# A fused attention and feed-forward step on one core: softmax-merge statistics on GpSimd, factor loads on SyncE, and the last merges inside the first output-projection block

## The chip, the cores and the metric

The kernel runs on one core of one Trainium2 chip. The metric is the device time of one execution in microseconds (us). The program is one launch of some 39,000 instructions on five engines, each of which works through its own instructions in order: TensorE (PE in the profile), VectorE (DVE), ScalarE (ACT), GpSimd (POOL) and SyncE (SP). SyncE issues most DMA transfers, ScalarE a few.

## The reference, cut to what matters

One layer for a prompt of 2048 positions and eight short samples: RMSNorm, one combined input projection, eight heads of attention with three dilated branches, a spatial gating unit, one output projection with a residual, and a SwiGLU feed-forward. All is in float32. What the change touches is the merge of the branches, per position and head:

```python
def _layer_prompt(x, biases, ...):
    q, k, v, u, vg = _project(x, norm1_g, w_in)
    for (w, d), bias_hj in zip(BRANCHES, biases):
        o, l = _dilated_prompt(q, k, v, bias_hj, d, w // d + 1)
        outs.append(o); lses.append(l)
    att = _merge_branches(outs, lses)
    ...
    x = x + jnp.concatenate([att, u * gate], axis=-1) @ w_out
    x = x + _swiglu(x, norm2_g, w_gate, w_up, w_down)

def _merge_branches(outs, lses):
    w = jax.nn.softmax(jnp.stack(lses, axis=0), axis=0)
    return jnp.sum(w[..., None] * jnp.stack(outs, axis=0), axis=0)
```

The kernel computes the two narrow branches together as a "band" and the widest one (distance 16) as a "strided" part, and merges the two results with two factors per position.

## The kernel before, in words

A float32 product is made of three products of high and low halves (`qh`, `ql`; `ph`, `pl`; `woh`, `wol`), so nearly every operand on its way to TensorE is split: ScalarE writes the high half, VectorE or GpSimd subtracts it.

**Phases.** The input projection ends about 599 us into the span. Then come the eight heads, until about 946 us; then the first block of the output projection (six tiles of 128 rows, the function `first_block`), and the feed-forward with its three blocks, which fills the rest.

**Attention items.** Each head has 20 items: 16 bands (128 queries against up to 640 keys) and 4 strided items (512 queries). One item is started per *step*; steps are counted from `B0`. A planner, `at(step, phase, function)`, sorts all the small functions by step, and within a step by phase (early, exp, low, scores, turn, mid, values, out, misc, store). That sorted list is the order of the instructions on every engine. A band takes: score matmuls (L881), the bias on VectorE (L887), the exponential on ScalarE (L892), transposes (L900), the copy of the high half `ph` (L903, ScalarE) and of the low half `pl` (L922, VectorE), and the product with the values (L936). A strided item has the like, with a max subtraction on GpSimd (`e`, L962), queries put in order by GpSimd (`qo`, L865), and its product with the values `v` at L985 and L986; ScalarE copies its result `o` out at L993. Items of a head follow a written list: `FIRST` for head 0, `OTHER` for heads 1 to 6, `LAST` for head 7.

**Merging a head.** When a head's items are over, during the next head's first steps, `Stats` spreads the strided sums (L1006, `sm`), sums them on TensorE (L1012) and copies them back (L1015). `Weights` forms the two factors (a minimum, a subtraction, an exponential, a product, a sum, a reciprocal, a product: L1030 to L1041), turns them (L1045) and stores them to a scratch array in memory, `f_d` (L1050, L1051). `merge_load` reads them back, spread over all partitions, in four chunks of 512 positions (`pair<-f_d`, L1061, issued on ScalarE's queue; `raw` and `zn`, L1065, on SyncE's queue for the last chunks). `merge` takes three instructions of GpSimd per chunk (L1072, L1074, L1076), one per step, and `merge_store` writes the rows of the head to `cat_d` (L1081).

**Loads of a head.** `load_head` issues on SyncE: `qh`, `k` and `ql` (L825, 1 MB each), the bias `b` (L830), and the values, `ve` for the bands (L836 or L845) and `v` for the strided items (L841, eight transfers). Head 0 does so during the end of the projection; head 1's loads begin at step 1 of head 0.

**Queues.** SyncE issues in order: a transfer that must wait (for its buffer, its data, or for the last transfer on its completion counter) holds all behind it. There are eight counters, taken in turn by the transfers of SyncE and ScalarE together.

**The first block.** Rows of `cat_d` are loaded per tile of 128 positions (`load_cat`, L1359) and split (`split_cat`, L1366 to L1370: a sum of halves into a staging tile `raw`, a copy on ScalarE, a subtraction on VectorE). The order of the tiles is 1, 2, the last slice of 1, 2 and 0, then 3, 4, 5 (first half of the columns), then the second half of the columns for all tiles, with weights `half1` (`fr<-in_w_out_dram`, 8 loads, L1332) that are split by ScalarE and GpSimd (L135, L138). `tick()` counts half tiles, and `later(n, ...)` puts work at such a tick.

Of the kernel before, what the change touches and what calls it, by code (L numbers as in the profile page):

```python
# [19 lines left out]
P = 128  # L20
T = 2048
# [44 lines left out]
def hymba_step(ctx: ExitStack, tc: tile.TileContext, A: dict, O: dict):  # L66
# [933 lines left out]
    class Stats:  # L1000
        def __init__(self, h, st):
            self.h, self.st = h, st["t"]

        def a(self):
            self.m = ap_.tile([P, 2 * P], F32, name="sm", tag="sm", bufs=1).rearrange("p (a r m) -> p a r m", a=2, m=RUN)
            dve.tensor_tensor(self.m, self.st[:, 4:6].unsqueeze(3).broadcast_to([P, 2, NT, RUN]),  # L1006
                              sel_m.unsqueeze(1).unsqueeze(1).broadcast_to([P, 2, NT, RUN]), op=OP.mult)
# [9 lines left out]
    class Weights:  # L1017
        def __init__(self, stats, n0=0, n1=NT):
            self.h, self.t, self.n0, self.n = stats.h, stats.st[:, :, n0:n1], n0, n1 - n0
# [7 lines left out]
        def weights_a(self):  # L1027

            self.f = f = self.small("f", 3)
            dve.tensor_tensor(f[:, 2, :], self.t[:, 0], self.t[:, 1], op=OP.min)  # L1030
            dve.tensor_sub(f[:, 0:2, :], self.both(f[:, 2:3, :]), self.t[:, 0:2])
            act.activation(f[:, 0:2, :], f[:, 0:2, :], AF.Exp)

        def weights_b(self):
            f, m = self.f, self.f[:, 2, :]
            dd = self.small("dd", 2)
            dve.tensor_mul(dd, f[:, 0:2, :], self.t[:, 2:4])
            dve.tensor_add(m, dd[:, 0, :], dd[:, 1, :])
            dve.reciprocal(m, m)
            self.w = w_ = self.small("w", 2)  # L1040
            dve.tensor_mul(w_, f[:, 0:2, :], self.both(self.f[:, 2:3, :]))  # L1041

        def turn(self):
            self.p = pt = ps_a()
            pe.transpose(pt[0:2 * self.n, 0:P], self.w.rearrange("p a t -> p (a t)"), ident)  # L1045

        def store(self):
            n = 2 * self.n
            rows = ap_.tile([2 * NT, P], F32, name="fr", tag="fr", bufs=2)[0:n]
# [6 lines left out]
    def merge_load(h, ch):  # L1056

        if h < H - 2 or h == H - 2 and ch < 2:
            f = pair_tile(F32)
            mf[h, ch] = (f[:, 0], f[:, 1])  # L1060
            act.dma_start(f, dap(f_d, h * 2 * T + ch * 512, [[0, P], [T, 2], [1, 512]]))  # L1061
# [55 lines left out]
    FIRST = list(range(8)) + ["s", 8, 9, "s", 10, 11, "s", 12, "s", 13, 14, 15]  # L1117
# [29 lines left out]
    for h in range(1, H):  # L1147

        s0 = B0 + (h - 1) * NI
        at(s0 + 1, "misc", begin, h)  # L1150
        for y in (1, 2, 3, 4, 10, 12):
            at(s0 + y, "misc", load, h)
        at(s0 + 16, "misc", order_bias, h)
    def stats_of(h, steps):
        d = {}
        at(*steps[0], lambda: d.update(s=Stats(h, sts[h])))
# [4 lines left out]
    def weights_of(d, steps, n0=0, n1=NT):  # L1161
        w = {}
        at(*steps[0], lambda: w.update(w=Weights(d["s"], n0, n1)))
        for (y, ph), fn in zip(steps, "weights_a weights_b turn store".split()):
            at(y, ph, lambda fn=fn: getattr(w["w"], fn)())

    def steps_of(s0, *steps):
        return [(s0 + y, ph) for y, ph in steps]

    for h in range(H):  # L1170
# [4 lines left out]
        if end:  # L1175

            x = s0 - NI
            d = stats_of(h, steps_of(x, (11, "misc"), (12, "early"), (13, "early")))
            weights_of(d, steps_of(x, (14, "early"), (14, "misc"), (16, "early"), (16, "exp")), 0, NT // 2)
            at(x + 17, "mid", merge_load, h, 0)  # L1180
            at(x + 17, "mid", merge_load, h, 1)
            for part in range(3):
                at(x + 19 + part, "store", merge, h, 0, dve, part)
                at(x + 20 + part, "store", merge, h, 1, pool, part)
            weights_of(d, steps_of(s0, (3, "early"), (4, "early"), (5, "early"), (5, "early")), NT // 2, NT)
        else:
            d = stats_of(h, steps_of(s0, (2, "misc"), (3, "misc"), (4, "early")))
            weights_of(d, steps_of(s0, (4, "misc"), (5, "misc"), (6, "turn"), (6, "mid")))

            for ch, (a, b) in enumerate(((8, 11), (8, 14), (14, 17), (20, 23) if ahead else (17, 20))):  # L1190
                at(s0 + a, "mid", merge_load, h, ch)
                for part in range(3):
                    at(s0 + b + part, "store", merge, h, ch, pool, part)
            if ahead:
                at(s0 + 17, "store", merge_store, h, 0, 2)
                at(s0 + 27, "store", merge_store, h, 2, 4)
            else:
                at(s0 + 23, "store", merge_store, h, 0, 4)
# [153 lines left out]
    def load_cat(B, i, a, b, place=None):  # L1352
# [7 lines left out]
        B.late[i, a] = (ch, cl, a, b)  # L1360

    def split_cat(B, i, a=0, staged=raw_tile):
        ch, cl, a, b = B.late.pop((i, a))
        m = max(a, 4)
        x = staged()[:, 0:(b - m) * P].rearrange("p (s t) -> p s t", t=P)
        dve.tensor_add(x, cl[:, m:b].bitcast(F32), ch[:, m:b].bitcast(F32))  # L1366
        for y0, y1, src in ((a, m, cl[:, a:m].bitcast(F32)), (m, b, x)):
# [424 lines left out]
    at(L + 1, "misc", split_cat, B, 0, 0, lambda: ap_.tile([P, 512], F32, name="m0", tag="m0", bufs=1))  # L1792
# [65 lines left out]
    def first_block(B):  # L1858

        places = {0: None, 1: acc_place(2), 2: acc_place(4)}  # L1860
# [5 lines left out]
        merge_load(h, 2)  # L1866
        merge_load(h, 3)
# [5 lines left out]
        load_cat(B, 4, 0, KD)  # L1873
        load_cat(B, 5, 0, KD)
        half1_load(*range(KD))
        sync.dma_start(gain[0], dap(A["final_g"], 0, [[0, P], [1, D]]))
        plan.run(10 ** 9)
        split_cat(B, 1)
        split_cat(B, 2)
        for n, what in ((2, [(merge, h, 2, pool), (merge, h, 3, pool), (split_cat, B, 1, KD - 1), (split_cat, B, 2, KD - 1)]),  # L1880
# [252 lines left out]
```

## Time and profile before

| what | value |
|---|---|
| median of 3 runs | 2623.61 us (2622.35 to 2627.72) |
| the profiled execution, its own time | 2621.67 us |
| its span in the profile | 2619.9 us |
| TensorE busy in the span | 2490.8 us (95%) |
| VectorE, ScalarE, GpSimd busy | 1425.6, 1221.1, 1370.9 us |
| the part that the change touches | about 590 to 1020 us of the span |
| TensorE busy in it | 386.16 of 430 us |

The time of the execution is 1.8 us more than the span. "Busy" of TensorE includes time in which its clock was granted at half speed, so the idle time alone doesn't say how much could be won. A row of waits names the engine and line that waited, what ended the wait last, the sum, the count and the longest. In a timeline each row has the start, the duration, the engine, the line, the output and input, and in brackets the idle time before it.

### The profile page before, as it was taken

Reading aid. Unit: us, or ns where it says so; the run is one execution under the profiler, and the core shown is the slowest. Engines: PE = TensorE matmul, PEld = TensorE weight load, DVE = VectorE, ACT = ScalarE, POOL = GpSimd, SP = SyncE. Lnnn points to the kernel's source line nnn. Section 1 sums busy time; section 2 is a strip of 40 time slices with the busy share of each in tenths; the row PEclk is TensorE's granted clock in tenths of the full one; section 3 lists DMA queues with packets and bytes.
Section 4 is the critical chain, followed back from the end, with each engine's and each line's share of the span. In section 5 each row is a group of like instructions: output and inputs, shape, how many; then the busy total and the mean of one; then the engine's idle time right before and its main releaser. Section 6 shows DMA issues by size and latency. Waiting matters only on the chain. (4 is left out here: it accounts for less than half of the span.)

```text
span 2619.9 us, 38931 instructions
## 1 busy us (share of the span) xinstructions
PE 2490.8 (95%) x13583; PEld 2202.5 (84%) x13583; DVE 1425.6 (54%) x2808; ACT 1221.1 (47%) x2570; POOL 1370.9 (52%) x1042
## 2 busy tenths in 40 slices
PE   8999899998999989999999999999999999999997
PEld 6777687677888868889989988999999987999996
DVE  3359686345888856444344465344444466444445
ACT  6424344445778746454554545332333336434332
POOL 2035754133567656776766743454554534666662
PEclk9999999999999989999999999899999999999999
DMA  8764844688677674464554664554453643655553
GB/s 245 224 203 153 279 147 129 183 263 241 187 227 226 165 217 141 155 194 146 181 177 133 197 177 140 169 186 172 152 210 129 224 148 125 200 198 195 198 199 110
DMA packets 313875, 481.06 MB, mean 184 GB/s; under 512 B 25907, under 2 KB 178916, under 8 KB 307792
## 3 DMA queue, kind: packets, MB, share of 16 engines
q1 hardware_dynamic: 301116, 455.90, 54.2%
q10 hardware_dynamic: 12564, 22.68, 3.3%
q8 instruction: 108, 1.77, 0.3%
q14 instruction: 87, 0.71, 0.1%
HBM read 382.76 MB, written 165.84 MB: 209 GB/s over the span
## 5 line engine op out<-in xcount | busy, mean ns | idle before, releaser
L1571 POOL TENSOR_TENSOR op<-fr,op 128x512 fp32r<-128x512 f32 x385 | 488.5, 1299 | 308.2 <-ACT op L1567 263.7
L1628 PE MATMUL ps_m<-xh,op 128*128 128x384 f32 (+4 forms) x1932 | 618.5, 320 | 3.8 <-DVE zn L1649 3.8
L1630 PE MATMUL ps_m<-xh,op 128*128 128x384 f32 (+4 forms) x1932 | 618.2, 320 | 1.7 <-POOL op L1571 1.7
L1629 PE MATMUL ps_m<-xl,op 128*128 128x384 f32 (+4 forms) x1932 | 617.3, 320 | 0.0
L1701 PE MATMUL ps_o<-dw,hw 128*128 128x512 f32 x2040 | 486.2, 393 | 18.2 <-DVE acc L1703 16.9
L1701 PEld LDWEIGHTS ps_o<-dw,hw 128*128 128x128 f32 x2040 | 380.4, 188 | 102.3 <-DVE acc L1703 24.0
L1628 PEld LDWEIGHTS ps_m<-xh,op 128*128 128x128 f32 x1932 | 371.9, 192 | 8.3 <-issue 2.8
L1629 PEld LDWEIGHTS ps_m<-xl,op 128*128 128x128 f32 x1932 | 371.6, 192 | 3.5
L1630 PEld LDWEIGHTS ps_m<-xh,op 128*128 128x128 f32 x1932 | 371.6, 192 | 2.0 <-POOL op L1571 2.0
L1703 DVE TENSOR_TENSOR acc<-acc,ps_o 128x512 f32<-128x512 f32 (+1 forms) x362 | 246.9, 686 | 215.1 <-PE ps_o L1701 215.0
L1668 ACT ACTIVATE ps_t<-zn 128x384 f32<-128x384 f32 (+1 forms) x126 | 58.3, 463 | 476.0 <-DVE zn L1651 370.4
L1567 ACT ACTIVATE op<-fr 128x512 fp32r<-128x512 f32 x396 | 235.4, 623 | 24.2 <-DMA fr<-ab_d 13.5
L138 POOL TENSOR_TENSOR dw<-fd,dw 128x1024 fp32r<-128x1024 f32 x66 | 158.7, 2405 | 123.3 <-ACT dw L135 123.1
L318 PE MATMUL ps_s<-wh,xh 128*128 128x512 f32 x480 | 198.4, 413 | 6.3 <-ACT xh L135 6.1
L319 PE MATMUL ps_s<-wl,xh 128*128 128x512 f32 x480 | 192.8, 402 | 1.7 <-DVE wl L226 1.7
L320 PE MATMUL ps_s<-wh,xl 128*128 128x512 f32 x480 | 192.3, 401 | 0.0
L1571 POOL TENSOR_TENSOR op<-pair,op 128x512 fp32r<-128x512 f32 x63 | 81.5, 1302 | 117.3 <-ACT op L1567 117.3
L1678 ACT ACTIVATE hw<-ps_t 128x384 fp32r<-128x384 f32 (+1 forms) x126 | 56.1, 453 | 175.3 <-DVE ps_t L1674 174.4
L318 PEld LDWEIGHTS ps_s<-wh,xh 128*128 128x128 f32 x480 | 93.0, 194 | 36.4 <-issue 8.2
L320 PEld LDWEIGHTS ps_s<-wh,xl 128*128 128x128 f32 x480 | 93.2, 194 | 20.8 <-DVE xl L138 0.2
L319 PEld LDWEIGHTS ps_s<-wl,xh 128*128 128x128 f32 x480 | 93.5, 195 | 20.2 <-DVE wl L226 2.6
L611 POOL TENSOR_TENSOR vl<-kv,vh 100x512 fp32r<-100x512 f32 (+1 forms) x32 | 46.1, 1440 | 109.9 <-ACT vh L605 35.7
(470 smaller groups left out, 4805.1 us busy)
## 6 DMA issues: line engine op xcount, KB each, us to landing
fr<-ab_d SPq DMA_DIRECT2D x308, 256.0 KB
fd<-in_w_down_dram SPq DMA_DIRECT2D x66, 512.0 KB
out_ks_dram<-in_cache_k_dram SPq DMA_DIRECT2D x56, 512.0 KB
out_vs_dram<-in_cache_v_dram SPq DMA_DIRECT2D x56, 512.0 KB
ab_d<-fr SPq DMA_DIRECT2D x88, 256.0 KB
raw<-in_w_in_dram SPq DMA_DIRECT2D x72, 256.0 KB
qk_d<-pair SPq DMA_DIRECT2D x64, 256.0 KB
ab_d<-pair SPq DMA_DIRECT2D x63, 256.0 KB
```

What stands on the lines that cost most here:

```text
L138: (eng_lo or pool).tensor_sub(lo, src, hi.bitcast(F32))
L318: pe.matmul(o[j], xh[:, k, :], wh, start=(k == 0), stop=False)
L319: pe.matmul(o[j], xh[:, k, :], wl, start=False, stop=False)
L320: pe.matmul(o[j], xl[:, k, :], wh, start=False, stop=(k == KD - 1))
L1567: act.activation(ops[f, j][0], ab[f][j], AF.Copy)
L1571: (pool if f or j in POOL_LOW else dve).tensor_sub(lo_, ab[f][j], hi.bitcast(F32))
L1628: pe.matmul(out, wh[:, ks], xh[:, :, k], start=(k == 0), stop=False)
L1629: pe.matmul(out, wh[:, ks], xl[:, :, k], start=False, stop=False)
L1630: pe.matmul(out, wl[:, ks], xh[:, :, k], start=False, stop=(k == 3))
L1668: act.activation(g, c, AF.Silu)
L1701: pe.matmul(ps[0:nr], l_, r_[:, cs], start=(z == 0 and y == 0), stop=(z == FC - 1 and y == len(pairs) - 1))
L1703: dve.tensor_add(B.acc[i][0:nr, cs], B.acc[i][0:nr, cs], ps[0:nr])
```

## The change

It has four parts.

1. **Statistics on GpSimd, and later.** For heads 0 to 6 five small operations (`sm`, the subtraction of `f`, the product `dd`, its sum, and `w`) go from VectorE to GpSimd. The minimum, the reciprocal and the copy of the sums stay on VectorE, the exponential on ScalarE. All are spread over more steps: the sums start at step 3 instead of 2, and the factors are stored at step 10 instead of 6. Head 7 keeps VectorE.
2. **Factor loads on SyncE, merges later.** The 26 loads `pair<-f_d` go from ScalarE's queue to SyncE's. The merges of a head start at steps 16, 19, 22 and 25 (before: 11, 14, 17, 20), its store is at 28 (before: 23).
3. **Head 0.** Its strided items come after bands 9, 11, 13 and 15 (before: after 7, 9, 11 and 12); head 1's loads start at step 6 instead of 1.
4. **The end.** Both early merges of head 7 are on GpSimd (one was on VectorE). Chunks 2 and 3 of head 6, which were merged during head 7, are merged in the first block, ahead of those of head 7; the second half of head 7's factors is turned and stored at tick 2 of the block instead of before it. The loads of tiles 4 and 5, the `half1` weights and `final_g` move behind head 6's store and head 7's factor loads. The split of tile 0 is in two parts.

```diff
         def a(self):
-            dve.tensor_tensor(self.m, self.st[:, 4:6].unsqueeze(3).broadcast_to([P, 2, NT, RUN]),
+            self.eng.tensor_tensor(self.m, self.st[:, 4:6].unsqueeze(3).broadcast_to([P, 2, NT, RUN]),
...
-            act.dma_start(f, dap(f_d, h * 2 * T + ch * 512, [[0, P], [T, 2], [1, 512]]))
+            sync.dma_start(f, dap(f_d, h * 2 * T + ch * 512, [[0, P], [T, 2], [1, 512]]))
...
-    FIRST = list(range(8)) + ["s", 8, 9, "s", 10, 11, "s", 12, "s", 13, 14, 15]
+    FIRST = list(range(10)) + ["s", 10, 11, "s", 12, 13, "s", 14, 15, "s"]
...
-            d = stats_of(h, steps_of(s0, (2, "misc"), (3, "misc"), (4, "early")))
-            weights_of(d, steps_of(s0, (4, "misc"), (5, "misc"), (6, "turn"), (6, "mid")))
+            d = stats_of(h, pool, steps_of(s0, (3, "misc"), (5, "early"), (6, "early")))
+            weights_of(d, steps_of(s0, (6, "misc"), (7, "early"), (7, "misc"), (8, "early"), (8, "misc"), (10, "early"), (10, "mid")))
+            chunks = ((13, 16), (13, 19), (19, 22), (22, 25))
...
     def first_block(B):
...
-        merge_load(h, 2)
-        merge_load(h, 3)
+        plan.run(10 ** 9)
+        split_cat(B, 1, 0, KD - 1)
+        split_cat(B, 2, 0, KD - 1)
         B.place()
...
-        load_cat(B, 4, 0, KD)
-        load_cat(B, 5, 0, KD)
-        half1_load(*range(KD))
...
-        for n, what in ((2, [(merge, h, 2, pool), (merge, h, 3, pool), (split_cat, B, 1, KD - 1), (split_cat, B, 2, KD - 1)]),
-                        (3, [(split_cat, B, 0, KD - 1), (split_cat, B, 3)]),
-                        (4, [(merge_store, h, 2, 4)]), (5, [(split_cat, B, 4), (open_end, B, 1)]),
+        for n, what in ((2, [(w.turn, lambda: ps_t(1)), (w.store, zn_tile), (merge_load, h - 1, 2), (merge_load, h - 1, 3)]),
+                        (3, [(split_cat, B, i, KD - 1) for i in (1, 2, 0)]),
+                        (4, [(merge, h - 1, 2, pool), (merge, h - 1, 3, pool), (merge_store, h - 1, 2, 4), (merge_load, h, 2), (merge_load, h, 3),
+                             (more_loads,), (split_cat, B, 3)]),
+                        (5, [(split_cat, B, 4), (open_end, B, 1)]),
+                        (6, [(merge, h, 2, pool), (merge, h, 3, pool), (merge_store, h, 2, 4), (half1_split, B, 0, 1)]),
```

What SyncE issues around head 0 (the rows are in the order of its queue; `-` stood there before, `+` stands there now):

```order
 L634 DMA cs_d<-zn 4x512
 L358 DMA v_d<-pair 128x1024
-L825 DMA qh<-qk_d 128x1x2048
 L350 DMA out_vp_dram<-zn 128x512 x2
-L825 DMA k<-qk_d 128x1x2048
 L358 DMA v_d<-pair 128x1024 x2
 L836 DMA ve<-v_d 128x6x128
+L841 DMA v<-v_d 16x16x128 x8
+L825 DMA qh<-qk_d 128x1x2048
+L825 DMA k<-qk_d 128x1x2048
 L825 DMA ql<-qk_d 128x1x2048
-L841 DMA v<-v_d 16x16x128 x8
```

Head 0's `v` now stands ahead of all three large loads of head 1.

GpSimd in the first steps of head 2, where the statistics of head 1 fall due, before:

```order
L1076 TENSOR_TENSOR ob<-ob,o_5763 128x512
L962 TENSOR_TENSOR e_6504<-e_6504,st 128x512
L865 COPY qo<-qh 128x512
L865 COPY qo<-ql 128x512
L962 TENSOR_TENSOR e_6637<-e_6637,st 128x512
L865 COPY qo<-qh 128x512
L865 COPY qo<-ql 128x512
L1072 TENSOR_TENSOR ob<-ob,pair 128x512
```

The same engine at the same kind of place now:

```order
L962 TENSOR_TENSOR e_6497<-e_6497,st 128x512
L1006 TENSOR_TENSOR sm<-st,sel_m 128x256
L1080 TENSOR_TENSOR o_5775<-o_5775,pair 128x512
L865 COPY qo<-qh 128x512
L865 COPY qo<-ql 128x512
L1082 TENSOR_TENSOR ob<-ob,o_5775 128x512
L1078 TENSOR_TENSOR ob<-ob,pair 128x512
L1031 TENSOR_TENSOR f<-f,st 128x32
L1080 TENSOR_TENSOR o_5775<-o_5775,pair 128x512
L1039 TENSOR_TENSOR dd<-f,st 128x32
L1040 TENSOR_TENSOR f<-dd 128x16
L1082 TENSOR_TENSOR ob<-ob,o_5775 128x512
```

The statistics of a head now run between the merge instructions of the head before it (`ob` and `o` with a factor; L1078, L1080 and L1082 are the old L1072, L1074 and L1076).

SyncE in the first block, behind the loads for tiles 0 to 2, before (`xl`, `xh` are the rows of a tile from `cat_d`, first tile 3, then 4 and 5; `acc` the residual rows of tiles 1 and 0):

```order
L1065 DMA raw<-f_d 128x512
L1065 DMA zn<-f_d 128x512
L1359 DMA xl_9904<-cat_d 128x128
L1359 DMA xh_9903<-cat_d 128x128
L1359 DMA xl_9904<-cat_d 128x8x128
L1359 DMA xh_9903<-cat_d 128x4x128
L1321 DMA acc_9909<-in_x_prompt_dram 128x1024
L1321 DMA acc_9911<-in_x_prompt_dram 128x1024
L1359 DMA xl_9904<-cat_d 128x8x128
L1359 DMA xh_9903<-cat_d 128x4x128
```

And now, from the same residual rows on, down to the load of tile 4:

```order
L1333 DMA acc_9895<-in_x_prompt_dram 128x1024
L1333 DMA acc_9897<-in_x_prompt_dram 128x1024
L1071 DMA raw<-f_d 128x512
L1071 DMA zn<-f_d 128x512
L1071 DMA raw<-f_d 128x512
L1071 DMA zn<-f_d 128x512
L1087 DMA cat_d<-ob 64x1024 x2
L1071 DMA raw<-f_d 128x512
L1071 DMA zn<-f_d 128x512
L1071 DMA raw<-f_d 128x512
L1071 DMA zn<-f_d 128x512
L1371 DMA xl_9890<-cat_d 128x8x128
```

The factor loads of head 6 stand behind the residual rows, and tile 4 behind head 6's store (`cat_d<-ob`), which waits for the last of six GpSimd merge instructions, and behind head 7's four factor loads. The residual row `acc_9895` shares its completion counter with the store of head 7's factors on ScalarE's queue, and waits for it.

111 lines of the change are left out of this document (62 added, 49 removed).

## The prediction

> **What bounds the kernel now.** I read the totals first, then the busy time by stretches, then what TensorE waited for in each stretch, then the timelines of those places. The totals and the stretches (length, then busy time of TensorE, its weight loads, VectorE, ScalarE, GpSimd, then TensorE's granted clock):
>
> ```profile
> PE 2490.8 (95%) x13583; PEld 2202.5 (84%) x13583; DVE 1425.6 (54%) x2808; ACT 1221.1 (47%) x2570; POOL 1370.9 (52%) x1042
> 800.00:850.00 50.00, 47.02 (x347) 44.23 (x345) 43.31 (x98) 39.79 (x95) 33.72 (x34) 0.97 0.79 227
> 920.00:940.00 20.00, 14.21 (x83) 11.95 (x82) 17.26 (x26) 12.41 (x31) 18.91 (x14) 0.88 0.75 190
> 940.00:960.00 20.00, 15.95 (x62) 12.22 (x62) 8.07 (x13) 3.63 (x8) 7.06 (x6) 0.84 0.54 155
> ```
>
> TensorE bounds the whole. In the heads VectorE is nearly as full (43.31 of 50 us), and GpSimd has room on average. At the end of attention TensorE is least busy, and GpSimd is full from 920 to 940. What TensorE waited for from 590 to 660, from 660 to 900 and from 900 to 1020 (sum, times, longest):
>
> ```profile
> PE ps_o L985 <- DMA v<-v_d: 5.2, 1, 5.2
> PE ps_t L900 <- DVE el L922: 1.4, 1, 1.4
> PE ps_o L900 <- DVE el L922: 1.0, 1, 1.0
> ...
> PE ps_o L936 <- ACT o L993: 4.4, 3, 2.0
> PE ps_t L1012 <- DVE pl L922: 3.4, 3, 1.4
> PE ps_o L1012 <- DVE pl L922: 1.9, 2, 1.1
> ...
> PE ps_t L900 <- DVE pl L922: 3.3, 2, 2.7
> PE ps_m L1380 <- DVE accm L1370: 3.3, 1, 3.3
> ```
>
> Waits are followed by stretches at half clock (the column 0.50):
>
> ```profile
> 631.40:638.20 6.80, 6.80 (x33) 6.80 (x33) 3.19 (x7) 2.79 (x6) 3.00 (x4) 0.50 1.22 222
> 706.50:709.90 3.40, 3.40 (x17) 3.40 (x16) 2.39 (x6) 2.16 (x5) 0.19 (x1) 0.50 0.96 235
> 733.80:737.20 3.40, 3.40 (x12) 2.81 (x13) 2.57 (x12) 1.16 (x4) 1.48 (x3) 0.50 1.02 393
> 812.10:815.50 3.40, 3.40 (x12) 2.83 (x12) 2.82 (x13) 2.32 (x7) 0.94 (x2) 0.53 1.04 352
> 853.10:856.50 3.40, 3.40 (x13) 3.16 (x12) 3.13 (x12) 2.29 (x7) 0.07 (x1) 0.53 1.03 286
> 935.20:942.00 6.80, 4.74 (x18) 4.29 (x19) 6.62 (x14) 1.68 (x4) 5.43 (x4) 0.50 0.77 195
> 955.70:962.50 6.80, 5.52 (x13) 4.38 (x14) 6.05 (x7) 0.72 (x3) 6.52 (x5) 0.50 1.08 335
> ```
>
> A busy microsecond at half clock loses half of itself: 3.4 us in the first row, 1.7 in each of the four rows of 3.40, 2.4 and 2.8 in the last two. The change is priced stage by stage, waits and clock together.
>
> **Term 1, head 0.** SyncE's timeline before:
>
> ```profile
> 600.69 1.19 SPq L825 DMA_DIRECT2D qh<-qk_d  x1
> 617.96 0.37 SPq L836 DMA_DIRECT2D ve<-v_d  x1
> 618.97 5.68 SPq L841 DMA_DIRECT2D v<-v_d  x8
> ```
>
> Head 0's `v` is issued late (618.97), and its first user waits 5.2 us for it. Head 1's `qh` (600.69) and `k`, 1 MB each, are issued ahead, in the time of the stores to `v_d` that `ve` waits for, and probably take bandwidth from them. The change takes both loads out of the way and puts two more bands, some 4 us of work at 2 us a step, ahead of the first strided product. Either would nearly do. The 5.2 us go, and the 3.4 us of half clock with them: 8.6. What is late next is VectorE, which these items already made wait 1.4 and 1.0 us. I take 8.6 - 2.4, so **6** (3 to 8.6).
>
> **Term 2, heads 1 to 6.** Loads on ScalarE's queue hold its copy `o`:
>
> ```profile
> 703.08 1.45 ACTq L1061 DMA_DIRECT2D pair<-f_d  x2
> 704.57 0.60 ACT L993 ACTIVATE o<-ps_o 128x512 f32<-128x512 f32 x1 [2.37 <-issue]
> ```
>
> The 4.4 us on `o` L993 go, and the 1.7 of half clock at 706.5. On SyncE I cost the 26 loads at nothing: they are due three steps (6 us) behind their store and three ahead of the merge. The head's store at step 28, which waits for the last merge, now stands ahead of the next `v`; those are needed some twelve steps later, which is the cover. The longer path to the factors meets merges that start five steps later too. The products of the statistics (L1012) waited 3.4 + 1.9 us in five heads behind VectorE, with three stretches of half clock (733.8, 812.1, 853.1) of 1.7: 10.4. They now go into TensorE's order at the start of a step instead of its end, a step and a bit behind `sm`, and VectorE has less to do:
>
> ```profile
> L1006 DVE TENSOR_TENSOR sm<-st,sel_m 128x256 f32<-128x256 f32 x6 | 5.8, 968 | 0.0
> L1031 DVE TENSOR_TENSOR f<-f,st 128x32 f32<-128x32 f32 x6 | 1.9, 314 | 0.2
> ```
>
> Up to 6.1 + 10.4 = 16.5 can go. Against it stands GpSimd. The groups of it from 660 to 900, six heads, and the products of the statistics by time:
>
> ```profile
> L1076 POOL TENSOR_TENSOR ob<-ob,o 128x512 f32<-128x512 f32 x24 | 31.2, 1300 | 0.5
> L962 POOL TENSOR_TENSOR e<-e,st 128x512 f32<-128x512 f32 x26 | 27.3, 1049 | 56.1 <-PE ps_t L900 34.1 <-DVE st L961 15.0 <-PE ps_o L900 7.0
> L865 POOL CAST qo<-qh 128x512 fp32r<-128x512 f32 x26 | 16.0, 614 | 0.0
> L854 POOL COPY bp<-b 128x640 f32<-128x640 f32 x6 | 7.9, 1316 | 0.0
> L1012 PE MATMUL ps_t<-sel_n,sm x16: 231/263/374, 733.6 to 890.8; 128*128 128x16 f32 x16
> ```
>
> 733.6 to 890.8 are four heads, so 39.3 us a head and 1.97 a step. In steps 16 to 27 GpSimd has twelve merge instructions (12 x 1.3 = 15.6), one `bp` (1.3), and three strided items (3 x (1.05 + 2 x 0.61) = 6.8): 23.7 us in twelve steps of 1.97 = 23.6. That was so before too, but now the statistics come on top. Their cost on GpSimd isn't in the trace: `sm` has half the columns of L962, hence some 0.55; the four small ones lie between nothing and L962's 1.05, and I take the 0.31 of the row L1031, which is one of them on VectorE. That makes 1.8, with ends of 0.5 and 4.8. So GpSimd gets about 2 us late at the end of the stretch, just where ScalarE's exponential needs `f` and VectorE's reciprocal needs the sum; both are in order, with the copies `ph` and `pl` for TensorE behind them. Of 2 us some 0.7 is covered by the distance of the phases. I charge 1.3 a head, 8 in six. **Term 2 is 16.5 - 8, about 8** (-6 to 16).
>
> **Term 3, end of attention.** VectorE merged a chunk of head 7, and one of its instructions there took 1.74 us:
>
> ```profile
> 934.77 1.74 DVE L1074 TENSOR_TENSOR o<-o,zn 128x512 f32<-128x512 f32 x1
> ```
>
> The wait of 2.7 us for `pl` and the half clock from 935.2 (2.4) lie right behind. Three merge instructions leave VectorE; the split of tile 0, cut in two, is the same work, and the gap between its halves is filled by the items' copies. GpSimd has as many chunks as before in the stretch. **5** (2 to 6).
>
> **Term 4, first block.** Rows of before, from GpSimd, SyncE, ScalarE, VectorE and TensorE:
>
> ```profile
> 953.39 1.27 POOL L1072 TENSOR_TENSOR ob<-ob,raw 128x512 f32<-128x512 f32 x1 [12.68 <-DMA raw<-f_d]
> 958.02 1.59 POOL L1072 TENSOR_TENSOR ob<-ob,raw 128x512 f32<-128x512 f32 x1
> 960.97 1.40 POOL L1076 TENSOR_TENSOR ob<-ob,o 128x512 f32<-128x512 f32 x1
> ...
> 941.34 7.92 SPq L1359 DMA_DIRECT2D accm<-cat_d  x4
> 949.30 0.43 SPq L1065 DMA_DIRECT2D raw<-f_d  x1
> ...
> 946.11 0.58 ACTq L1051 DMA_DIRECT2D f_d<-fr  x1
> ...
> 966.02 0.39 PE L1378 MATMUL ps_m<-op,xh 128*128 128x512 f32 x1
> 981.66 0.39 PE L1378 MATMUL ps_m<-op,xh 128*128 128x512 f32 x1
> ```
>
> 69 products in 15.64 us are 0.227 us each, 24 of them a half tile (5.45). Counted from the first product of tile 1, TensorE without waits is at the last slice of tile 0 at +10.9, at tile 3 at +11.6, at tile 4 at +17.0. Now the chain that feeds them. The factors of head 7 are turned after 12 products (+2.7), and their store is issued at about +3.6. Before, a store issued at 946.11 let SyncE go on at about 948.0 (the four loads end at 949.26, three issues of 0.43 behind the release). So +5.6, and then, at 0.45 an issue, two residual rows and head 6's factors at +7. They took 4.1 us (949.30 to 953.39); behind 1 MB of residual rows I take 5, so GpSimd starts at +12. By the rows its first merge instruction is done 1.3 later, its fourth 6.2, its sixth 9.0.
>
> The staging tile for tile 0's last slice waits for the first instruction (+13.3; split by +14.4, a wait of 3.5), that of tile 3 for the fourth (+18.2; split by +19.6 against +15.1, 4.5). Tile 4's load stands behind the store that waits for the sixth (+21), two issues of 0.55 and four of 0.47: +24, landed and split by +30, against +27: 3. These are 11 us, and three stretches of half clock of about 2 each: 17. What goes is the 3.3 us on L1380 and its 2.8 at half clock, 6. **Term 4 is -11** (-22 to 0).
>
> **Sum.** 6 + 8 + 5 - 11 = 8 us. From the profiled execution, 2621.67, this gives 2613.7; the median of the runs lies 1.9 above that execution. I predict **2614**.
>
> [...]
>
> **Rivals.**
> - *GpSimd becomes the bound of the heads* (slower). Place: the subtraction `f` and the sum on GpSimd, due at steps 6 and 7. If `f` and the sum are late by 2 us each time and TensorE then waits 2.6 in all and drops its clock (1.7), a head loses 4.3, six lose 26: 16.5 - 26 = -9.5 for term 2, and 6 - 9.5 + 5 - 11 = -9.5: **2631**. It decides from 3.6 us a head on. For it: 23.7 of 23.6 us. Against: the L962 row's 56.1 us of idle time ahead.
> - *The first block's queue costs more.* If the factors land at +16 and tile 4 takes 8 us from its issue (twice the 4.1 above), the waits are 7.5, 4.5 and 6.6 and term 4 is -19: **2622**.
> - *Half clock doesn't follow the waits.* Without the four short stretches term 2 is about 1: **2621**. [...]
> - *GpSimd stays hidden, or the first block's waits hide one another* (each makes the next one's need later). One of the two: **2604**.
>
> **How the numbers follow.** Forecast 0.38 (2607 to 2618), hidden costs 0.22, the queue 0.17, the clock 0.08, GpSimd as the bound 0.15. The range 2601 to 2629 leaves out most of the last and the edge of the second. A measurement of this kernel can tell about 0.2% (5.2 us) from no change, here 2618.4 to 2628.9: faster 0.60, same 0.25, slower 0.15.
>
> **What would show it.** Term 1: no wait of L985 for `v` near 631. Term 2: no waits on `o` L993 or at the statistics' products; instead some for the exponential and the reciprocal behind GpSimd, and a head of about 38 us instead of 39.3. Term 3: 920 to 940 fuller. Term 4: SyncE's residual row waits for ScalarE's store, GpSimd starts about 12 us after the first product of tile 1, and TensorE waits at tiles 0, 3 and 4. I am wrong if the heads don't shorten, or if the first block loses less than 5 us or more than 20.

## The result and the profile after

Over 20 runs each, the changed kernel takes 2624.25 us (2619.62 to 2633.17) and the kernel before 2622.59 us (2610.49 to 2629.59). The ratio is 1.0015, with a 95% interval of 1.0001 to 1.0029: no change by the bound of 0.2%, and if anything slower. I had forecast 2614. The profiled execution of the changed kernel has a span of 2621.9 us.

Where the time went is read best from one event that both kernels have in the same order: the copies of the band result `ob` on ScalarE, four per head, and behind them the first product of tile 1 in the first block and the first product of its second half (`woh`). Two such rows of before, the second copies of heads 1 and 6:

```profile
679.51 0.60 ACT L945 ACTIVATE ob<-ps_o 128x512 f32<-128x512 f32 x1
877.39 0.60 ACT L945 ACTIVATE ob<-ps_o 128x512 f32<-128x512 f32 x1
```

The same two in the changed kernel:

```profile
669.81 0.60 ACT L945 ACTIVATE ob<-ps_o 128x512 f32<-128x512 f32 x1
863.76 0.60 ACT L945 ACTIVATE ob<-ps_o 128x512 f32<-128x512 f32 x1
```

Such times, from one profiled execution of each kernel (before, changed, and four of the experiments below; the rows of "from there" and "to" are lengths):

| event | before | changed | part 3 | parts 1, 2 | part 4 | parts 1 to 3 |
|---|---|---|---|---|---|---|
| head 0, first `ob` | 616.08 | 616.50 | 618.60 | 618.36 | 618.90 | 622.50 |
| head 1, second `ob` | 679.51 | 669.81 | 673.60 | 677.86 | 683.22 | 675.70 |
| from head 0's first `ob` to that | 63.43 | 53.31 | 55.00 | 59.50 | 64.32 | 53.20 |
| five heads, to head 6's second `ob` | 197.88 | 193.95 | 199.81 | 192.90 | 197.15 | 194.03 |
| from there to tile 1's first product | 70.52 | 73.80 | 71.61 | 77.13 | 66.35 | 79.50 |
| from there to the second half | 34.43 | 54.42 | 33.17 | 34.46 | 53.68 | 33.96 |

The first row differs by up to 6.4 us, although what TensorE computes up to there is the same in all six. So absolute times of different kernels are not compared below, only lengths from one event to the next.

The change wins 10.1 us from the first `ob` to head 1 (9.7 from the start of the span), 3.9 in five heads, loses 3.3 up to the first block and 20.0 in it. By the second half it is 9.6 us late. Some 8 us of that come back in this pair of profiles behind 1640 us, where nothing was changed; the last section says what that is.

**Head 0.** The wait for `v` is gone (from 590 to 660 no wait of TensorE in the changed kernel is longer than 1.0 us). Before, two stretches at a clock of 0.50 stood there, 6.8 us each, from 631.4 and from 651.9; in the changed kernel one of 3.4 us at 0.50 is left, from 635.1.

**The five heads.** The five heads as one stretch, before and in the changed kernel:

```profile
679.51:877.39 197.88, 183.78 (x1337) 172.90 (x1337) 171.72 (x390) 154.53 (x362) 124.89 (x126) 0.97 0.77 224
669.81:863.76 193.95, 180.26 (x1337) 165.99 (x1337) 164.97 (x365) 153.76 (x362) 129.80 (x149) 1.00 0.79 223
```

TensorE's busy time is the second number, its granted clock the third from the end. It does the same 1337 products. Its idle time, length less busy time, is 14.1 us before and 13.7 now, so the waits bring 0.4; its busy time is 3.5 us shorter, and the clock, 0.97 before, is full. What TensorE waited for in these two stretches, before:

```profile
PE ps_o L936 <- ACT o L993: 4.4, 3, 2.0
PE ps_t L1012 <- DVE pl L922: 3.4, 3, 1.4
PE ps_t L900 <- DVE el L922: 2.7, 10, 0.6
PE ps_o L1012 <- DVE pl L922: 1.9, 2, 1.1
PE ps_o L900 <- DVE el L922: 1.1, 5, 0.4
```

And in the changed kernel:

```profile
PE ps_t L900 <- DVE el L922: 3.8, 10, 0.5
PE ps_t L1012 <- POOL sm L1006: 2.3, 3, 0.8
PE ps_o L900 <- DVE el L922: 1.8, 5, 0.5
PE ps_t L900 <- ACT e L892: 1.6, 5, 0.4
PE ps_t L1051 <- DVE pl L922: 1.5, 3, 0.5
PE ps_o L1051 <- DVE pl L922: 1.0, 2, 0.5
PE ps_o L900 <- ACT e L892: 0.8, 2, 0.4
PE ps_o L1012 <- POOL sm L1006: 0.8, 1, 0.8
```

The waits on `o` and for VectorE at L1012, 9.7 us, have gone, and others of 9.8 us stand in their place: for GpSimd at L1012 (3.1), at the turn of the factors, L1051 (2.5), for `e` (2.4), and 1.8 more for `el`.

**The end.** The waits from 900 to 1020 in the changed kernel:

```profile
PE ps_m L1392 <- ACT xh L1383: 14.1, 2, 8.0
PE ps_m L1394 <- DVE xl L1384: 3.6, 2, 2.9
PE ps_o L985 <- ACT o L993: 2.6, 1, 2.6
PE ps_t L1051 <- DVE w L1047: 1.9, 1, 1.9
```

The first two rows are the first block: 17.7 us, where before had 3.3 on L1380. The stretches from 920 on:

```profile
920.00:940.00 20.00, 17.45 (x102) 14.35 (x101) 14.65 (x26) 11.79 (x27) 12.21 (x10) 1.00 0.61 158
940.00:960.00 20.00, 12.00 (x49) 9.18 (x48) 4.72 (x9) 2.25 (x6) 4.83 (x4) 0.81 0.61 188
960.00:980.00 20.00, 10.23 (x27) 6.80 (x27) 5.75 (x6) 1.89 (x3) 10.52 (x9) 0.67 0.75 177
```

From 940 to 980 TensorE is busy for little more than half (22.23 of 40 us), at a clock of 0.81 and 0.67.

### The profile page after: what moved, and what is told of

It reads as the page before. It is cut to its first block, busy times and chain, and to the rows that moved or that the text cites. A ratio compares the mean times of both kernels' runs of the same rounds, so it can differ in the third digit from the quotient of the medians.

```text
span 2621.9 us, 38941 instructions
## 1 busy us (share of the span) xinstructions
PE 2480.9 (95%) x13583; PEld 2188.5 (83%) x13583; DVE 1414.6 (54%) x2770; ACT 1221.5 (47%) x2570; POOL 1382.9 (53%) x1080
## 5 line engine op out<-in xcount | busy, mean ns | idle before, releaser
L1715 PEld LDWEIGHTS ps_o<-dw,hw 128*128 128x128 f32 x2040 | 381.1, 189 | 102.1 <-DVE acc L1717 23.8
```

What stands on the lines that cost most here:

```text
L1715: pe.matmul(ps[0:nr], l_, r_[:, cs], start=(z == 0 and y == 0), stop=(z == FC - 1 and y == len(pairs) - 1))
```

## The experiments

All changes are against the kernel named. Every ratio is to the kernel before, run in the same session. "Stretch" is the time from tile 1's first product to the first product of the second half.

**The parts one by one.** Part 3 alone, on the kernel before:

```diff
-    FIRST = list(range(8)) + ["s", 8, 9, "s", 10, 11, "s", 12, "s", 13, 14, 15]
+    FIRST = list(range(10)) + ["s", 10, 11, "s", 12, 13, "s", 14, 15, "s"]
-        at(s0 + 1, "misc", begin, h)
+        at(s0 + (6 if h == 1 else 1), "misc", begin, h)
...
+            y = int(h == 0)
+            d = stats_of(h, steps_of(s0 + y, (2, "misc"), (3, "misc"), (4, "early")))
```

> The kernel before with part 3 alone (head 0's strided items and head 1's loads later; head 0's statistics and merges one step later, since its last item now ends later). Theory 1, each part acts in its own place: the wait for v near 631 and its half clock go, head 1 starts about 9.7 us earlier as in the trace of the changed kernel, and nothing is given back: about 9 us faster in the median (6 to 11). Rival, the clock and the order of the items give it back in the heads: head 1 starts earlier, and tile 1's first product less than 4 us earlier; under 4 us faster.

Measured: 2608.81 us (2603.61 to 2613.05) against 2619.21, ratio 0.9954 (0.9936 to 0.9973): 12 us faster by the ratio, above the forecast of 9. In the profile the way from the first `ob` to head 1 is 8.4 us shorter (head 1 itself is only 5.9 earlier, since this execution reached the first `ob` 2.5 us later). The five heads take 1.9 more, the way to tile 1 takes 1.1 more, and the stretch is 1.3 shorter. That is 6.7 us; the rest comes behind the places of the change, so the profile places only part of what the many runs show.

Parts 1 and 2 alone:

```diff
-            d = stats_of(h, steps_of(s0, (2, "misc"), (3, "misc"), (4, "early")))
+            d = stats_of(h, pool, steps_of(s0, (3, "misc"), (5, "early"), (6, "early")))
...
-            act.dma_start(f, dap(f_d, h * 2 * T + ch * 512, [[0, P], [T, 2], [1, 512]]))
+            sync.dma_start(f, dap(f_d, h * 2 * T + ch * 512, [[0, P], [T, 2], [1, 512]]))
...
+        if ahead:
...
+            chunks = ((10, 12), (10, 15), (14, 18), (20, 23))
+        else:
...
+            chunks = ((13, 16), (13, 19), (19, 22), (22, 25))
```

> The kernel before with parts 1 and 2 alone (statistics of heads 0 to 6 on GpSimd and later, factor loads on SyncE, merges later; head 6's four chunks stay in head 7, the first block and head 0 as before). Theory 1: five heads, from the second copy of the band result of head 1 to that of head 6, take 2 to 5 us less than the 197.9 us of before, since throttle-free heads take 38.7 to 39.5 us in both kernels; 0 to 5 us faster in all. Rival, the statistics on GpSimd are what costs the 3 to 4 us lost in heads 6 and 7: then tile 1's first product is not earlier than before (947.9) and the median is 0 to 4 us slower.

Measured: 2615.67 us, ratio 0.9997 (0.9977 to 1.0017). The five heads take 5.0 us less (192.90), as theory 1 had it, and the stretch from head 6 to tile 1 takes 6.6 us more (77.13), as the rival had it. Both are so, and in the ratio they cancel: what the heads win is lost again between head 6 and tile 1. With the old end, head 6's later factors probably crowd head 7; no run moved them alone. TensorE's waits from 880 to 948 in this kernel begin with

```profile
PE ps_t L900 <- DVE pl L922: 5.2, 2, 3.1
```

Part 4 alone (the changed kernel with the rest undone):

```diff
-            d = stats_of(h, pool, steps_of(s0, (3, "misc"), (5, "early"), (6, "early")))
+        d = stats_of(h, dve, steps_of(s0, (2, "misc"), (3, "misc"), (4, "early")))
+        chunks = ((10, 13), (10, 16)) if ahead else ((8, 11), (8, 14), (14, 17), (17, 20))
-            sync.dma_start(f, dap(f_d, ...))
+            act.dma_start(f, dap(f_d, ...))
```

> The kernel before with part 4 alone (the end: head 7's early merges on GpSimd, head 6's last chunks in the first block, loads of tiles 4 and 5 behind them; statistics on VectorE and factor loads on ScalarE's queue as before). Theory 1, the first block's queue is the whole loss: from tile 1's first product to the first product of the second half 50 to 56 us instead of 34.4, with waits at tiles 0, 3 and 4 of 15 us or more in sum: 15 to 22 us slower. Rival, the loss needs the late factors of part 1: the stretch takes under 45 us and the kernel is under 10 us slower.

Measured: 2630.73 us, ratio 1.0052 (1.0032 to 1.0072), 14 us slower by the ratio and just below the forecast of 15 to 22. The stretch takes 53.68 us, as in the changed kernel; the statistics have no part in it. From head 6 to tile 1 it is 4.2 us faster than before, which is what term 3 was about.

Parts 1 to 3 with the old end (the statistics as in the run of parts 1 and 2):

```diff
-            act.dma_start(f, dap(f_d, h * 2 * T + ch * 512, [[0, P], [T, 2], [1, 512]]))
+            sync.dma_start(f, dap(f_d, h * 2 * T + ch * 512, [[0, P], [T, 2], [1, 512]]))
...
+    FIRST = list(range(10)) + ["s", 10, 11, "s", 12, 13, "s", 14, 15, "s"]
```

> The changed kernel with part 4 undone (parts 1, 2 and 3). Theory 1, the parts add up: the sum of the two runs above, 9 to 14 us faster than before (the changed kernel's heads were 13.6 us ahead at head 6). Rival: head 6's late factors and the fuller GpSimd hurt the end also with the old order there, and under 6 us remain.

Measured: 2612.37 us, ratio 0.9977 (0.9959 to 0.9996): 6 us faster, at the rival's bound; theory 1, that the parts add up to 9 to 14, failed. From head 6 to tile 1 it takes 79.50 us, 9.0 more than before. By the ratios part 3 gives -12, parts 1 and 2 about -1, part 4 +14. Their sum, +1, agrees with the changed kernel's 1.0015 (3.9 us, 0.3 to 7.6), but with intervals of some 5 us to either side of each it could hardly have failed to, and parts 1 to 3 together give 6, not 13.

**The first block.** What holds TensorE at tile 4? The loads moved ahead, on the changed kernel (e_cat_ahead):

```diff
-                        (2, [..., (merge_load, h - 1, 2), (merge_load, h - 1, 3)]),
+                        (2, [..., (merge_load, h - 1, 2), (merge_load, h - 1, 3), (more_loads,)]),
...
-                             (more_loads,), (split_cat, B, 3)]),
+                             (split_cat, B, 3)]),
```

> The changed kernel with one thing moved: the loads of tiles 4 and 5, the half1 weights and final_g are issued at tick 2, behind head 6's factor loads but ahead of head 6's store and head 7's factor loads. Theory 1, tile 4 waits for SyncE's order: its wait of 6.2 us and some of the half clock behind it (3.4) go, the waits at tiles 0 and 3 (8.0 and 2.9) stay; from tile 1's first product to the second half 44 to 49 us instead of 54.4, 5 to 10 us faster than the changed kernel. Rival, GpSimd's six merge instructions are the limit anyway (tile 4's staging tile waits for head 7's first one): the wait at tile 4 stays over 4 us and the stretch over 50 us.

Measured: ratio 1.0028 (1.0005 to 1.0051) against before; the stretch is 52.99 us. Theory 1 failed, the rival holds: tile 4's rows are issued 16 us earlier (950.67 instead of 966.91) and the wait stays. VectorE's row for its split and TensorE's for the tile, in this kernel:

```profile
974.68 1.77 DVE L1380 TENSOR_TENSOR raw<-xl,xh 128x512 f32<-128x512 f32 x1 [10.71 <-POOL ob L1078]
...
978.18 0.79 PE L1394 MATMUL ps_m<-op,xl 128*128 128x512 f32 x1 [7.64 <-DVE xl L1384]
```

The split needs a staging tile `raw`, of which there are three, and head 7's factors sit in it until GpSimd's first merge instruction on them.

The order mended, on the changed kernel:

```diff
         load_acc(B, 0)
+        load_cat(B, 4, 0, KD)
+        load_cat(B, 5, 0, KD)
...
-        for n, what in ((2, [(w.turn, lambda: ps_t(1)), (w.store, zn_tile), (merge_load, h - 1, 2), (merge_load, h - 1, 3)]),
-                        (3, [(split_cat, B, i, KD - 1) for i in (1, 2, 0)]),
+        for n, what in ((2, [(w.turn, lambda: ps_t(1)), (w.store, zn_tile)]),
+                        (3, [(split_cat, B, i, KD - 1) for i in (1, 2, 0)] + [(split_cat, B, 3), (merge_load, h - 1, 2), (merge_load, h - 1, 3), (more_loads,)]),
```

> The changed kernel with the first block's order mended: the loads of tiles 4 and 5 behind the residual rows, then the last slices' and tile 3's splits, which so take staging tiles that no merge holds, and only then head 6's factor loads and the half1 weights; the merges stay in the block. Theory 1: no wait at tiles 0, 3 and 4 over 1.5 us, the stretch from tile 1's first product to the second half 29 to 37 us instead of 54.4, about 15 to 20 us faster than the changed kernel and some 13 to 18 faster than before. Rival, the half1 weights become late behind twelve merge instructions on GpSimd: the waits move to the second half, and under 10 us come back.

Measured: ratio 1.0033 (1.0015 to 1.0051). The waits at tiles 0 and 3 are gone (0.8 left), and the wait at tile 4 grows to 10.2 us, tile 5 waits 3.1: the merges come later, and with them the staging tiles. The stretch is 48.71 us. My forecast of 29 to 37 was wrong, because I had left tiles 4 and 5 on `raw`.

A staging tile of the splits' own, on the kernel with the loads ahead:

```diff
+        def own():
+            return fl.tile([P, 256], F32, name="own", tag="own", bufs=1)
+        def split(i):
+            split_cat(B, i, 0, 6, own)
+            split_cat(B, i, 6, KD, own)
...
-                             (split_cat, B, 3)]),
-                        (5, [(split_cat, B, 4), (open_end, B, 1)]),
+                             (split, 3)]),
+                        (5, [(split, 4), (open_end, B, 1)]),
```

> The kernel of e_cat_ahead (loads of tiles 4 and 5 and half1 weights ahead of head 6's store) with a staging tile of its own, half as wide, for the splits of tile 0's last slice and of tiles 3, 4 and 5, which are done in two pieces; so no split waits for a merge. Theory 1: the waits at tiles 0, 3 and 4 (7.9, 2.9, 7.6) fall to under 2 us each, but the second half then waits for GpSimd: it has twelve merge instructions (some 17 us) ahead of the first half1 split, which came at 982.7 in e_cat_ahead, 44.5 us after the first product of tile 1, where TensorE would be at +28. So one wait of 8 to 16 us on woh, and the stretch still 42 to 50 us. Rival, with the staging tiles free the merges are off the path: the stretch is 29 to 36 us and the kernel is 10 us or more faster than before.

Measured: ratio 1.0016 (1.0002 to 1.0030). The waits at tiles 0, 3 and 4 fall to 0.3, 0.6 and 3.9 with 1.0. GpSimd's first `half1` split and TensorE's second product of the second half, in this kernel:

```profile
983.61 2.50 POOL L138 TENSOR_TENSOR woh<-fr,woh 128x512 fp32r<-128x512 f32 x2
...
984.93 0.80 PE L1393 MATMUL ps_o<-woh,pair 128*128 128x512 f32 x1 [7.31 <-POOL woh L138]
```

The second half starts 37.1 us after tile 1 (42 to 50 expected) and stops at once for 7.3 us (8 to 16 expected), so its second product comes at 44.8. The split comes 43.5 us after tile 1's first product, since it stands behind twelve merge instructions in GpSimd's order. Yet GpSimd isn't full: in front of head 7's six it idles for 11.75 us. That is most likely the wait for head 7's factors, whose loads stand behind head 6's store; in the kernel with the loads ahead the same wait, 10.57 us, ends with such a load. So theory 1 had the place right, and what holds is order more than GpSimd's speed. Three things hold the block one behind another: SyncE's order, the staging tiles, and the splits behind the merges on GpSimd. A kernel with the splits ahead of head 7's merges wasn't run. With six merges in the block (before, and parts 1 to 3) the stretch is 34 us.

**What paces the heads.** Six kernels put extra work into the changed kernel, per strided item; measured are the five heads (193.95 us there), in one execution each. Three more profiles with the same heads, those of the experiments on the first block, have 192.28, 192.39 and 192.67, so a difference of under 2 us says nothing. The edits stand in this order: at the bias on VectorE (e_dve_more), the scores on TensorE (e_pe_more), the copy `eh` on ScalarE (e_act_more), the queries on GpSimd (e_pool_more), then, when those had shown ScalarE's price, the low half `el` on VectorE (e_el_more) and copies ahead of `eh` on ScalarE (e_act_aside):

```diff
+        for _ in range(2):
+            dve.tensor_reduce(st[:, 5, r4 * 4:r4 * 4 + 4], e, axis=AX.X, op=OP.min)
...
-        for a in range(4):
+        for a in (0, 1, 2, 3, 0, 1, 2, 3):
...
-        act.activation(eh, pt, AF.Copy)
+        for _ in range(3):
+            act.activation(eh, pt, AF.Copy)
...
-        for z, q in enumerate(("qh", "ql")):
+        for z, q in ((0, "qh"), (1, "ql"), (0, "qh"), (1, "ql")):
...
-        it.update(eh=eh, el=el, lo=[(el, pt, eh)])
+        it.update(eh=eh, el=el, lo=[(el, pt, eh)] * 3)
...
+        for _ in range(2):
+            act.activation(eh, it["e"].rearrange("p a b -> p (a b)"), AF.Copy)
```

> The changed kernel with two more reductions on VectorE per strided item (2 x 0.68 us, 5.4 us a head; the results are overwritten). Measured is the stretch of heads 1 to 6 (second copy of the band result in head 1 to the second in head 6: 193.95 us in the changed kernel, five heads). Theory A, VectorE sets the pace of a head: about +25 us (5 a head). Theory B, TensorE does, and VectorE has the slack that its 85% busy time shows: under +8 us.

> The changed kernel with the score products of the strided items done twice (8 products, some 1.0 us per item, 4 us a head; same result). Theory A, VectorE sets the pace: under +6 us over the five heads. Theory B, TensorE sets it: about +20 us.

> The changed kernel with the copy of the strided items' high half on ScalarE done three times (2 x 0.6 us more, 4.8 us a head). If ScalarE has slack (40 of 50 us busy), under +8 us over the five heads; if the items wait for its copies in order, +15 us or more.

> The changed kernel with the queries of the strided items put in order twice (2 x 0.61 us more, 4.9 us a head). The rival of the prediction, GpSimd becomes the bound of the heads: +15 us or more over the five heads, with waits for qo, sm and w. If GpSimd has room over a whole head (36.6 of 50 us busy): under +8 us.

> The changed kernel with the low half el of the strided items subtracted three times (2 x 0.68 us more on VectorE per strided item, 5.4 us a head, at a place where TensorE waits for el; e_dve_more had the same amount elsewhere, +8.9 us over the five heads). Theory L, the heads are paced by the round from TensorE's transposes over ScalarE's copy and VectorE's subtraction back to TensorE: +20 us or more over the five heads. Theory S, ScalarE's instruction stream itself is the limit and VectorE has room: about +9, as in e_dve_more.

> The changed kernel with two more copies on ScalarE per strided item that need nothing from the transposes (the exponentials copied into eh, overwritten by the real copy at once): 4.8 us a head as in e_act_more (+23.8 us over the five heads), but ahead of the copy that TensorE's next bank waits for, in time in which ScalarE partly waits for the transposes. Theory L: clearly less than in e_act_more, 5 to 15 us. Theory S, ScalarE's stream is the limit: +20 us or more.

| extra work | engine | amount in five heads | five heads take | more | of it TensorE's idle time | TensorE's clock |
|---|---|---|---|---|---|---|
| reductions at the bias | VectorE | 27 us | 202.84 | 8.9 | 8.6 | 1.00 |
| scores twice | TensorE | 18 us | 195.66 | 1.7 | -10.9 | 1.00 |
| copy `eh` three times | ScalarE | 24 us | 217.74 | 23.8 | 16.4 | 0.95 |
| queries twice | GpSimd | 25 us | 203.57 | 9.6 | 2.7 | 0.96 |
| `el` three times | VectorE | 28 us | 219.82 | 25.9 | 19.3 | 0.95 |
| copies ahead of `eh` | ScalarE | 25 us | 203.40 | 9.5 | 8.9 | 0.98 |

The amounts are the number of extra instructions by their duration in the profiles; for the scores, which overlap, it is the growth of their rows' busy time (39.1 us instead of 21.2). What isn't idle time is longer busy time, in three of the rows some 7 us, where the clock fell. Nearly the same amount on VectorE cost 8.9 in one place and 25.9 in another, and on ScalarE 23.8 and 9.5; in idle time alone 8.6 and 19.3, 16.4 and 8.9. So no engine's total sets the price. It fits the round trip from TensorE's transposes over ScalarE's copy and VectorE's subtraction back to TensorE, whose next transposes wait for `el` (5.6 us in the five heads of the changed kernel): work on it cost nearly all it took (25.9 of 28 us, 23.8 of 24), work beside it about a third (8.9 of 27, 9.5 of 25). TensorE's waits from 670 to 860 with `el` three times:

```profile
PE ps_t L900 <- DVE el L922: 17.3, 10, 2.5
PE ps_o L900 <- DVE el L922: 10.5, 6, 2.4
```

Of the first two, theory A (VectorE sets the pace, 25 us) failed in the first with 8.9, and theory B (TensorE does, 20 us) in the second with 1.7: the added products went into TensorE's idle time, of which 2.8 us were left. The copy `eh` (15 or more if the items wait for it) came at 23.8, and GpSimd's 9.6 lies between its two forecasts, 15 or more as the bound and under 8 with room. Theory L of the last two, which is the round trip, had 20 or more and 5 to 15, and got 25.9 and 9.5.

**Part 3 with the factor loads on SyncE**, statistics as before:

```diff
-            act.dma_start(f, dap(f_d, ...))
+            sync.dma_start(f, dap(f_d, ...))
```

> Part 3 alone (2608.8 us, ratio 0.9954) plus the factor loads on SyncE, with the statistics on VectorE and the merges where they were. Theory: ScalarE's copies are on the chain that paces the heads (an added us of them cost a us), so its waits at the loads (4.4 us on o in the profile before) count, and the five heads take 2 to 5 us less than in part 3 alone (199.8): ratio 0.993 to 0.995. Rival: the loads on SyncE wait for the store of the factors, 2 steps earlier than in the changed kernel, and hold the values' loads; the heads take as long or longer, ratio 0.996 or more.

Measured: ratio 0.9960 (0.9945 to 0.9975), the same as part 3 alone (0.9954) within the intervals, and at the rival's bound. The wait on `o` (8.1 us in part 3's profile) is gone from this one, and the five heads take 196.06 us, 3.8 less, as the theory had it; the ratio doesn't show it. It stays open whether the loads bring anything.

## Why the prediction was wrong, step by step

In short: against the forecast, the traces differ by +3.7 us in term 1, -4.1 in term 2, -8.3 in term 3 and -9.0 in term 4. So the forecast of 8 us faster failed most on what the pushed work holds up at the end: on the size of the first block's waits, and on a cost between head 6 and tile 1 that had stood at nothing.

- **Term 1 (6 us): right in mechanism, too small.** The wait for `v` went and most of the half clock with it; the way to head 1 became 10.1 us shorter in the changed kernel and 8.4 in part 3 alone, which gave 12 us by the ratio. I had priced one of the two stretches at half clock, and the deduction for VectorE (2.4 us) wasn't due.
- **Term 2 (8 us): the step that failed is to count the waits that go as gain, and the half clock at half of its busy time.** I had 9.7 us of waits and 6.8 of clock, 16.5 in all, less 8 for GpSimd. The five heads take 3.9 us less. The waits went as I had said and brought 0.4, since others of 9.8 us came, of which 3.1 are GpSimd's `sm` and the rest are not GpSimd's. The half clock went too: the four stretches are gone, and TensorE's busy time for the same products fell by 3.5 us and not by 6.8. Why it fell by half only, no run shows.
- **Term 3 (5 us): right in itself; what failed is that the cost of the late factors of head 6 stood at nothing.** From head 6 to tile 1 part 4 gives 4.2 us alone, and 5.7 on top of parts 1 to 3 (73.80 against 79.50). But parts 1 and 2 alone cost 6.6 us there, and together with part 4 it is a loss of 3.3. The waits that the changed kernel has there, and part 4 alone has not, are mainly those for `o` (2.6) and for GpSimd at `w`, `qo` and `sm` (1.6, 1.0, 0.8). I had counted GpSimd's chunks at this place, and not what its later factors hold up.
- **Term 4 (-11 us): the mechanism was right, the size was not.** It is -20.0. All three waits came where I had put them, at tiles 0, 3 and 4: 8.0, 2.9 and 6.2 us instead of 3.5, 4.5 and 3. The two stretches, before and changed:

```profile
947.91:982.34 34.43, 31.13 (x124) 24.95 (x124) 16.84 (x22) 10.28 (x20) 15.43 (x12) 0.90 0.88 270
937.56:991.98 54.42, 35.73 (x124) 26.69 (x125) 17.81 (x22) 10.63 (x21) 26.30 (x21) 0.78 0.73 210
```

  Of the 20.0 us 15.4 are idle time (3.3 before, 18.7 now; I had 7.7 net) and 4.6 longer busy time. What was mis-sized is first the start of GpSimd, +17.5 instead of +12 (955.09 against 937.56), then the way of tile 4's rows. The chain in the changed kernel, ScalarE's store, SyncE's loads, GpSimd's first merge, then the second round:

```profile
942.24 0.59 ACTq L1057 DMA_DIRECT2D f_d<-zn  x1
...
947.92 0.65 SPq L1071 DMA_DIRECT2D raw<-f_d  x1
963.13 1.09 SPq L1087 DMA_DIRECT2D cat_d<-ob  x2
966.91 1.72 SPq L1371 DMA_DIRECT2D xl<-cat_d  x1
...
955.09 1.26 POOL L1078 TENSOR_TENSOR ob<-ob,raw 128x512 f32<-128x512 f32 x1 [16.48 <-DMA raw<-f_d]
970.82 1.28 POOL L1078 TENSOR_TENSOR ob<-ob,raw 128x512 f32<-128x512 f32 x1 [7.72 <-DMA raw<-f_d]
...
958.12 0.80 PE L1392 MATMUL ps_m<-op,xh 128*128 128x512 f32 x1 [8.00 <-ACT xh L1383]
963.70 0.79 PE L1394 MATMUL ps_m<-op,xl 128*128 128x512 f32 x1 [2.93 <-DVE xl L1384]
977.89 0.79 PE L1392 MATMUL ps_m<-op,xh 128*128 128x512 f32 x1 [6.15 <-ACT xh L1383]
```

  The store is at +4.7 (I had 3.6), the factor loads at +10.4 (7, the loads for tiles 0 and 3 stand in the queue too), and they take 7.2 us (5) behind tile 3's rows and the residual rows. Tile 4's rows, issued at 966.91, are split by 977.9: 11.0 us, where I had 6. The half clock cost little more than I had said, 4.6 us of busy time against 6 less 2.8. What I had not seen is that mending one of these only shows the next.
- **The sum** of terms 1 to 4 as traced is 9.7 + 3.9 - 3.3 - 20.0 = -9.7, so 9.7 us slower; the ratio says 3.9 slower (0.3 to 7.6). The traces are single executions, and what separates the two figures isn't placed. The forecast also left out the 1.9 us by which it had put the median above the profiled execution; with them it would have been 2615.6.
- **The rivals.** "The first block's queue costs more" (2622) came nearest, in place and in price (-19 against -20.0). That its time came near too is luck: with the traced gains in the other terms (10.3 us instead of 19) it would have been some 9 us more. My chance for it was 0.17, and 0.60 for faster was too high. GpSimd as the bound of the heads didn't come: 25 us more on it cost 9.6, of which 2.7 were idle time of TensorE. "Half clock doesn't follow the waits" didn't come for the heads: in all six profiles that have the new statistics and no extra work the five heads run at a clock of 1.00, in the four with the old ones at 0.96 to 0.98.
- **What would show it.** No wait for `v` came, as written, and from 920 to 940 TensorE is fuller (17.45 instead of 14.21). In the heads the waits on `o` went, but at the statistics' products VectorE was only replaced by GpSimd, and "a head of about 38 us" didn't come (38.8 instead of 39.6). In the first block the three waits came, with GpSimd at +17.5 instead of about +12; the loss of 20.0 us lies at the bound of 20 that I had set.

## What to carry to other kernels

Before waits are added up as a gain, find what paces the loop: add a known amount of work at two places of the same engine and see which one costs its full price. Here added work cost nearly all it took on that chain (23.8 of 24 us) and about a third beside it (9.5 of 25), so work taken off elsewhere can pay as little, and a wait removed can come back as another (9.7 us of waits went in the heads, others of 9.8 came). To see whether it did, compare TensorE's idle and busy time between the same two events of both kernels, not in windows at the same time. And when work is pushed into a later stage, count there what it holds while it waits (queue order, staging tiles, the engine), since mending the first alone shows the next.

## What the runs showed of the hardware

The waits alone didn't settle the granted clock here. At the same place of the feed-forward the two profiles have the same wait, 1.18 and 1.19 us, before:

```profile
1639.73 0.30 PE L1628 MATMUL ps_m<-xh,op 128*128 128x128 f32 x1 [1.18 <-DVE zn L1649]
```

and after:

```profile
1648.97 0.30 PE L1642 MATMUL ps_m<-xh,op 128*128 128x128 f32 x1 [1.19 <-DVE zn L1663]
```

Before was then at a clock of 0.50 for 17.1 us, from 1641.8, although from 1600 to 1660 TensorE has no longer wait than that of 1.18 us; the changed kernel was at 1.00 there. The stretches of before:

```profile
1640.00:1650.00 10.00, 10.00 (x57) 10.00 (x56) 2.80 (x8) 4.38 (x10) 5.47 (x5) 0.59 0.36 116
1650.00:1660.00 10.00, 10.00 (x45) 10.00 (x45) 2.23 (x8) 3.19 (x8) 3.49 (x3) 0.56 0.59 202
```

and of after:

```profile
1650.00:1660.00 10.00, 10.00 (x86) 10.00 (x86) 5.30 (x15) 5.06 (x13) 7.50 (x6) 1.00 0.56 184
```

That is worth some 8 us, two thirds of what part 3 gives. Of the sixteen profiles, which do the same work there, five have such a stretch of 17 or 20 us at this place and eleven have none. Whether a change shifts how often it comes, single profiles can't say. So two profiles can't be compared by their spans here, only by stretches, and a difference of a few us needs many runs.
